# Three projection spans behind the last gate block, with SiLU built from Exp, and memory pools in another order

## The chip, the core and the metric

One core of a Trainium2 chip runs the whole kernel in one launch. The metric is the time on the device in microseconds (us). Three runs of the kernel before gave 1357.52, 1358.02 and 1362.52 us; their median, 1358.02 us, is the time before. The engines are named as the profile names them: PE (TensorE, matmuls and transposes), DVE (VectorE), ACT (ScalarE), POOL (GpSimd) and SP (SyncE, which here issues nearly all DMAs, in program order).

## The reference, cut to what matters

The layer normalises 2048 prompt tokens and 64 sample tokens, projects them with one weight matrix, runs differential attention and a convolution branch beside each other, multiplies each by its own gate, and projects the result back.

```python
h = rmsnorm(yp, norm_g[l])
q, k, v, g_att, u, g_conv = in_project(h, w_in[l])      # z = h @ w_in, split
o = lax.map(q_block, jnp.arange(n_blocks))              # diff_attend, causal, 128 queries each
att = attn_post(o, subln_g[l], lam_init)
conv, buf_p = conv_branch(u, zero_buf, *conv_p)         # depthwise conv, layernorm, silu, w_pw2
m = concatenate([att * silu(g_att), conv * silu(g_conv)], axis=-1)
yp = yp + m @ w_out[l]
```

All data are fp32. The change concerns `silu(g_conv)` for the last 128 of the 1024 gate channels, and the start of the attention.

## The kernel before, in words

**Phase 1** projects. The normalised input lies in SBUF, transposed, as a high and a low part (`hH`, `hL`) in four token groups of 512, 512, 512 and 576 tokens. `zmm` multiplies a block of 128 output channels with one span of tokens: 8 slices of the contraction times three products (high by high, low by high, high by low) are 24 matmuls that add up in one PSUM bank. A block has five spans (`SPANS`): three of 512 and two of 288 tokens. `zbank` takes the PSUM bank from a ring of pools, so that neighbouring spans lie in different banks. The last part of phase 1 is eight gate blocks. `gate_block(i)` computes for each span `zmm`, one ACT instruction `Silu` from PSUM into a tile `eF`, and one DMA of that tile to a DRAM tensor `gd[i]`. The layernorm of the convolution (`ln_steps`) runs between the spans of blocks 0 to 6.

**Phase 2** is attention. Scores `S` (lines 616 and 617) go from PE into two PSUM tiles of two banks each; DVE copies each to SBUF with a running minimum (lines 638 and 641); ACT takes the exponential (line 649); POOL and DVE combine the two softmaxes (lines 655 and 661); PE transposes (678), ACT copies (683), PE multiplies with the values (696). A group is one head and 512 queries. The first group (head 0, queries 0 to 511) has its keys `kt`, values `vt` and queries `qt` loaded during the gate blocks, into a pool of their own. Those of the second and third group (queries 512 to 1023 and 1024 to 1535) are loaded at the seam between the phases, from DRAM, into memory that `hH` and `hL` give back. `pw_stream` (weights `pwr`, split into `pwH` and `pwL`) is the pointwise convolution; it runs in low priority beside attention.

A scheduler sets the order of the instructions on each engine once, when the kernel is built: it follows the order in which the code records them, moved by `high_priority` offsets (a negative offset lets an instruction stand later). On the chip each engine and SP's DMA queue then go through their own list in that order, and an instruction whose semaphore is not yet up holds everything behind it on its engine. A PSUM or SBUF tile can be written again only after the last reader of its former content.

## Time and profile before

| | |
|---|---|
| median of three runs | 1358.02 us |
| profiled execution, its own time | 1358.04 us |
| its span, first to last instruction | 1356.3 us |
| PE busy | 1289.4 us, 95% of the span |
| DVE busy | 865.9 us, 64% |
| ACT busy | 517.2 us, 38% |
| mean granted PE clock | 0.989 |

The span is the time between the first and the last instruction of the profiled execution; its own time is 1.7 us longer. Times in the trace are microseconds from the start of the span. The seam between the phases lies at 692 us. A granted clock of 1.0 means 2.4 GHz for PE, and 0.5 means 1.2 GHz.

### The profile page before, as it was taken

What the parts mean: (1) busy time and instruction counts of PE and PEld (TensorE: products, weight loads), DVE (VectorE), ACT (ScalarE), POOL (GpSimd) and SP (SyncE); (2) the same over time, 40 slices, a digit from 0 to 9 for tenths busy, and PEclk for the clock granted to TensorE, in tenths of its full rate; (3) what the DMA queues carried; (4) which work ended last, traced back from release to release, by engine and by line L of the source; (5) the groups of instructions that cost most, each with busy time, mean ns of one, the idle gap of its engine ahead of it and who ended that gap; (6) DMA issues with size and microseconds to landing.
All of it is one profiled execution on the core that took longest, in us unless ns stands there. A gap on an engine that the chain in (4) does not pass through costs nothing.

```text
span 1356.3 us, 19981 instructions
## 1 busy us (share of the span) xinstructions
PE 1289.4 (95%) x7552; PEld 1105.1 (81%) x7552; DVE 865.9 (64%) x1215; ACT 517.2 (38%) x949; POOL 249.5 (18%) x353
## 2 busy tenths in 40 slices
PE   6999999999999999999988999999989779999997
PEld 5897998998888888888876888888877567767776
DVE  6623998998999992333137778777777935214332
ACT  6622111211212222323247666656767645212221
POOL 3200200200201100000024223224234425401110
PEclk9999999999999999999989999999999989999999
DMA  7632231330432336433166455363164544567731
GB/s 259 202 122 63 75 124 34 102 113 25 126 111 68 142 134 184 134 121 107 68 150 177 122 148 148 102 168 102 44 162 155 155 133 134 190 204 272 245 128 63
DMA packets 127858, 180.23 MB, mean 133 GB/s; under 512 B 25234, under 2 KB 74642, under 8 KB 127762
## 3 DMA queue, kind: packets, MB, share of 16 engines
q1 hardware_dynamic: 127762, 178.96, 43.8%
q8 instruction: 59, 0.97, 0.3%
q14 instruction: 37, 0.30, 0.1%
HBM read 113.88 MB, written 65.04 MB: 132 GB/s over the span
## 4 chain that ended last, share of the span: by engine, by line
PE 80%; DMA 8%; DVE 4%; ACT 2%; issue 2%; SPq 2%; POOL 1%; DVEq 0%; POOLq 0%; ACTq 0%
PE zps L204 39%; PE yps L974 13%; PE zps L328 7%; PE O L696 6%; PE pt L551 3%; PE S L616 3%; PE pt L678 3%; PE S L617 3%; DMA wor<-in_wout 2%; DMA kt<-kd 2%; DVE pL L661 1%; DVE pL L638 1%; DMA qt<-qd 1%; PE dO L763 1%; DMA wr<-in_wz 1%
## 5 line engine op out<-in xcount | busy, mean ns | idle before, releaser
L204 PE MATMUL zps<-hH,wH 128*128 128x512 f32 (+2 forms) x984 | 343.7, 350 | 3.9 <-ACT wH L160 3.9
L204 PE MATMUL zps<-hL,wH 128*128 128x512 f32 (+2 forms) x984 | 343.3, 349 | 0.0
L204 PE MATMUL zps<-hH,wL 128*128 128x512 f32 (+2 forms) x984 | 343.3, 349 | 0.0
L241 DVE SCALAR_TENSOR_TENSOR acc<-u,cst,acc 128x1024 f32<-128x1024 f32 x240 | 313.2, 1332 | 6.9 <-ACT acc L239 4.1
L204 PEld LDWEIGHTS zps<-hH,wH 128*128 128x128 f32 x984 | 185.5, 189 | 26.4 <-ACT wH L160 4.7
L204 PEld LDWEIGHTS zps<-hH,wL 128*128 128x128 f32 x984 | 185.7, 189 | 21.5
L204 PEld LDWEIGHTS zps<-hL,wH 128*128 128x128 f32 x984 | 185.4, 188 | 21.4
L974 PE MATMUL yps<-wo,mH 128*128 128x512 f32 x544 | 179.0, 404 | 6.2 <-ACT wo L1017 5.1
L616 PE MATMUL S<-kt,qt 128*128 128x512 f32 (+3 forms) x320 | 130.1, 410 | 20.3 <-DVE pL L638 6.9
L696 PE MATMUL O<-at,vt 128*128 128x256 f32 (+1 forms) x576 | 142.5, 375 | 0.6 <-ACT at L683 0.5
L974 PEld LDWEIGHTS yps<-wo,mH 128*128 128x128 f32 x544 | 101.9, 189 | 35.5 <-ACT wo L1017 5.3
L649 ACT ACTIVATE pL<-pL,mn 128x1152 f32<-128x1152 f32 (+7 forms) x64 | 104.3, 1630 | 37.3 <-DVE mn L641 36.9
L617 PE MATMUL S<-kt,qt 128*128 128x512 f32 (+3 forms) x320 | 114.3, 368 | 0.0
L696 PEld LDWEIGHTS O<-at,vt 128*128 128x128 f32 x576 | 103.1, 194 | 11.8 <-ACT at L683 1.1
L974 PE MATMUL yps<-wo,mL 128*128 128x512 f32 x272 | 108.5, 399 | 0.0
L683 ACT ACTIVATE at<-pt 128x512 f32<-128x512 f32 (+1 forms) x144 | 78.9, 567 | 56.0 <-PE pt L678 54.6
L616 PEld LDWEIGHTS S<-kt,qt 128*128 128x128 f32 x320 | 60.6, 190 | 41.2 <-DVE pL L638 11.2
L638 DVE TENSOR_SCALAR_CACHE_REDUCE pL<-S 128x1024 f32<-128x1024 f32 x64 | 78.1, 1220 | 23.1 <-PE S L617 22.5
L641 DVE CUSTOM_DVE_ANT_0 pS<-S,trim 128x768 f32<-128x768 f32 (+7 forms) x64 | 47.3, 754 | 63.0 <-PE S L617 61.1
L661 DVE SCALAR_TENSOR_TENSOR pL<-pL,cf,pL 128x512 f32<-128x512 f32 (+2 forms) x112 | 80.3, 774 | 10.5 <-POOL cf L656 10.2
L977 DVE TENSOR_TENSOR y<-yps,y 128x512 f32<-128x512 f32 (+1 forms) x34 | 23.2, 689 | 88.9 <-PE yps L974 66.0
L655 POOL TENSOR_TENSOR cf<-sm,mone 128x1 f32<-128x1 f32 x64 | 40.0, 625 | 215.8 <-ACT pL L649 112.6
(163 smaller groups left out, 1948.0 us busy)
## 6 DMA issues: line engine op xcount, KB each, us to landing
qt<-qd SPq DMA_DIRECT2D x32, 512.0 KB, 7.2
wr<-in_wz SPq DMA_DIRECT2D x48, 256.0 KB, 3.3
kt<-kd SPq DMA_DIRECT2D x38, 256.0 KB, 5.6
xt<-in_xp SPq DMA_DIRECT2D x16, 512.0 KB, 5.3
mf<-md SPq DMA_DIRECT2D x8, 1024.0 KB, 7.0
y<-in_xp SPq DMA_DIRECT2D x16, 512.0 KB, 5.0
kr<-in_ck SPq DMA_DIRECT2D x32, 256.0 KB, 4.5
vr<-in_cv SPq DMA_DIRECT2D x32, 256.0 KB, 4.9
```

The costliest lines, as they stand in the source:

```text
L204: PE.matmul(ps[:, 0:n], lhsT=wt[:, ks], rhs=ht[g][:, k, off:off + n], start=(i == 0), stop=(i == 3 * KC - 1))
L241: DVE.scalar_tensor_tensor(out=a, in0=u[:, t:t + HS], scalar=dwwt[:, cg, t:t + 1], in1=a, op0=ALU.mult, op1=ALU.add)
L328: PE.matmul(ps[0:n, 0:256], lhsT=ht[g][:, k, off:off + n], rhs=wt[:, sl], start=(i == 0), stop=(i == 3 * KC - 1))
L616: PE.matmul(ps[:, o:o + n], lhsT=t["mq"][:, m, qs_], rhs=kk, start=True, stop=False)
L617: PE.matmul(ps[:, o:o + n], lhsT=t["mq"][:, 2 + m, qs_], rhs=kk, start=False, stop=True)
L638: DVE.tensor_scalar(out=dst, in0=ps, scalar1=0.0, scalar2=None, op0=ALU.add, op1=ALU.min, accum_out=mn[:, m, 0:1])
L641: DVE.tensor_tensor_reduce(out=dst, in0=ps[:, 0:w], in1=trim[:, 1024 - w:] if diag else trim[:, 0:1].to_broadcast([P, w]), scale=1.0, scal ...
L649: ACT.activation(q, q, AF.Exp, bias=B["mn"][:, m, c:c + 1], scale=-1.0, accum_out=B["sm"][:, m, B["i"] % 4:B["i"] % 4 + 1])
L661: DVE.scalar_tensor_tensor(out=p0, in0=p1, scalar=B["cf"], in1=p0, op0=ALU.mult, op1=ALU.add)
L683: ACT.activation(at[:, 0:n * P], pt[:, 0:n * P], AF.Copy)
L696: PE.matmul(O[:, dst], lhsT=vt[j // 4][:, j % 4, :], rhs=at[:, src], start=(j == 0), stop=part)
L974: PE.matmul(ps, lhsT=m[:, k, sl], rhs=wo[k][x][:, cs], start=(i == 0), stop=(i == 3 * KC - 1))
```

## The change

`gate_block` gets an argument `late`. For the last block (i = 7) it is 3: the first two spans stay as they were, and the last three (512, 288 and 288 tokens; called late spans A, B and C from here) are recorded under `high_priority(offset=-LOW)`, with PSUM pool `psg` alone, which has one bank. Their SiLU is no longer one ACT instruction but a chain of four: Exp on ACT (from PSUM into `eF`), add 1 on DVE, reciprocal on DVE, and the product with the PSUM bank on DVE. The ACT table for Exp and Ln is loaded ahead of them instead of at the start of phase 2. The pools of both phases are opened in another order, so that the addresses of `hH`, `hL`, the weight ring and phase 2's tiles lie differently over each other. The rest of the code is the same.

```diff
-    hpool = ph1.enter_context(tc.tile_pool(name="hT", bufs=1))
     wpool = ph1.enter_context(tc.tile_pool(name="wring", bufs=3))
     wraw = ph1.enter_context(tc.tile_pool(name="wraw", bufs=2))
+    hpool = ph1.enter_context(tc.tile_pool(name="hT", bufs=1))
     epool = ph1.enter_context(tc.tile_pool(name="evac", bufs=5))
-    psz = ph1.enter_context(tc.tile_pool(name="psz", bufs=4, space=PSUM))
-    zps = [psz] * 4
-    hH = [hpool.tile([P, KC, n], F32R, name=f"hH{g}") for g, n in enumerate(GW)]
-    hL = [hpool.tile([P, KC, n], F32R, name=f"hL{g}") for g, n in enumerate(GW)]
+    psg = ph1.enter_context(tc.tile_pool(name="psg", bufs=1, space=PSUM))
+    psz = ph1.enter_context(tc.tile_pool(name="psz", bufs=3, space=PSUM))
+    zps = [psz, psz, psz, psg]
+    hH, hL = [None] * 4, [None] * 4
+    for g in (3, 0, 1, 2):
+        hH[g] = hpool.tile([P, KC, GW[g]], F32R, name=f"hH{g}")
+        hL[g] = hpool.tile([P, KC, GW[g]], F32R, name=f"hL{g}")
...
-    def gate_block(i, slots=()):
+    def gate_block(i, slots=(), late=0):
         w = wprep(wz[(8 if i < 4 else 16) + i])
-        for j, (g, off, n) in enumerate(SPANS):
+
+        def span(g, off, n, act):
+            ps = zmm(w, g, off, n)
+            f = ev(F32, "eF")
+            act(f[:, 0:n], ps[:, 0:n])
+            t0 = tokens(g, off)
+            SP.dma_start(gd[i][:, t0:t0 + n], f[:, 0:n])
+
+        def silu_exp(f, ps):
+            ACT.activation(f, ps, AF.Exp, scale=-1.0)
+            DVE.tensor_scalar(out=f, in0=f, scalar1=1.0, scalar2=None, op0=ALU.add)
+            DVE.reciprocal(out=f, in_=f)
+            DVE.tensor_tensor(out=f, in0=ps, in1=f, op=ALU.mult)
+
+        for sp in SPANS[0:len(SPANS) - late]:
             if len(slots):
                 for f in slots.pop(0):
                     f()
-            ps = zmm(w, g, off, n)
-            f = ev(F32, "eF")
-            ACT.activation(f[:, 0:n], ps[:, 0:n], AF.Silu)
-            t0 = tokens(g, off)
-            SP.dma_start(gd[i][:, t0:t0 + n], f[:, 0:n])
+            span(*sp, lambda f, ps: ACT.activation(f, ps, AF.Silu))
+        if late:
+            tc.keep_in_program_order(ACT.preload_act_table_set("natural_log_exp_and_others"))
+            zps[:] = [psg]
+            with tc.high_priority(offset=-LOW):
+                for sp in SPANS[len(SPANS) - late:]:
+                    span(*sp, silu_exp)
...
-        gate_block(i, slots)
+        gate_block(i, slots, 3 if i == 7 else 0)
...
+    st = pool2("st", 8)
     ppS = pool2("ppS", 1)
-    kp = pool2("kp", 2)
-    qp = pool2("qp", 2)
-    vp = pool2("vp", 2)
     ap_ = pool2("ap", AB)
     op = pool2("op", 2)
-    st = pool2("st", 8)
+    qp = pool2("qp", 2)
+    kp = pool2("kp", 2)
+    vp = pool2("vp", 2)
...
-    tc.keep_in_program_order(ACT.preload_act_table_set("natural_log_exp_and_others"))
```

How it moves the instructions is seen at three places. First PE, at the end of the last gate block. Before, the last matmuls `zps` of the block's last span stand directly ahead of the first four score matmuls `S`, and the second score pair (128x256) follows them:

```order
L204 MATMUL zps<-hH_138,wL 128x288
L204 MATMUL zps<-hL_142,wH 128x288
L616 MATMUL S<-kt_7066,qt 128x128 [waits DMAHW6_49,DMAHW3_49,DMAHW7_49,DMAHW2_49,Activation_49]
L616 MATMUL S<-kt_7066,qt 128x128 [waits DVE_49]
L617 MATMUL S<-kt_7066,qt 128x128 x2
L616 MATMUL S<-kt_7066,qt 128x256 [waits DVE_49]
L617 MATMUL S<-kt_7066,qt 128x256
```

Of the change, the end of late span A (512 columns) and the start of late span B (288 columns):

```order
L207 MATMUL zps<-hH_144,wH 128x512
L633 MATMUL S<-kt_7079,qt 128x128 [waits DMAHW6_49,DMAHW3_49,DMAHW7_49,DMAHW2_49,Activation_49]
L633 MATMUL S<-kt_7079,qt 128x128 [waits DVE_49,Activation_49]
L634 MATMUL S<-kt_7079,qt 128x128 x2
L207 MATMUL zps<-hH_144,wL 128x512
L207 MATMUL zps<-hL_145,wH 128x512
L207 MATMUL zps<-hH_138,wH 128x288 [waits DVE_49]
L207 MATMUL zps<-hH_138,wL 128x288
```

The first four score matmuls moved ahead of the last two matmuls of span A. All 48 matmuls of spans B and C follow without another instruction between them, and the second score pair (128x256) stands behind them, where it stood before. The first matmul of B, and likewise that of C, waits for DVE.

Second DVE, at the same place. `eF` is the SiLU chain, and the rows at L658 (before: L641) are the score minima of the first tiles:

```order
L355 TENSOR_SCALAR eF<-eF 128x512 [waits DMAHW0_49,Activation_49]
L356 RECIPROCAL eF<-eF 128x512 [waits DVE_49]
L357 TENSOR_TENSOR eF<-zps,eF 128x512 [waits DVE_49]
L355 TENSOR_SCALAR eF<-eF 128x288 [waits DMAHW2_49,DMAHW1_49,Activation_49]
L356 RECIPROCAL eF<-eF 128x288 [waits DVE_49]
L357 TENSOR_TENSOR eF<-zps,eF 128x288 [waits DVE_49]
L658 ISA pS_7103,mn<-S,trim 128x128 [waits PE_49]
L658 ISA mn 128x1
```

The chains of A and B stand ahead of the first score minimum; before, nothing of the gate block was on DVE there. The chain of C follows between the next minima.

Third SP's DMA queue, which stores the gate tiles `gd` and loads keys, values and queries. Before:

```order
L350 DMA gd_85<-eF 128x512 [waits DMAHW6_49,Activation_49]
L350 DMA gd_85<-eF 128x288 [waits DMAHW7_49,Activation_49]
L710 DMA kt_7074<-kd_64 64x2x512 [waits DMAHW0_49,PE_49]
L710 DMA kt_7074<-kd_64 64x2x512 [waits DMAHW1_49]
L712 DMA vt_7077<-vd 128x4x128 [waits DMAHW2_49,PE_49]
L719 DMA qt<-qd_60 64x4x512 [waits DMAHW3_49]
```

Of the change:

```order
L351 DMA gd_85<-eF 128x512 [waits DMAHW6_49,DVE_49]
L351 DMA gd_85<-eF 128x288 [waits DMAHW7_49,DVE_49]
L727 DMA kt_7087<-kd_64 64x2x512 [waits DMAHW0_49,PE_49]
L727 DMA kt_7087<-kd_64 64x2x512 [waits DMAHW1_49]
L729 DMA vt_7090<-vd 128x4x128 [waits DMAHW2_49,PE_49]
L736 DMA qt<-qd_60 64x4x512 [waits DMAHW3_49]
```

The loads of the second group keep their place behind the stores of spans A and B; those stores now wait for DVE's product instead of ACT's Silu. The PE wait of `vt` was for the last span (its memory was `hL3`) and is now for span A (`hH2`). Further down the queue the load of `pwr` moved behind the queries of the fourth group (it stood ahead of them), and on ACT the first split of `pwr` moved behind the first exponential of 1152 columns.

## Rows read from the trace of the kernel before

**Rows 1.** The page: busy time of each engine with its share of the span and instructions, and the chain of work that ended last, as shares of the span by engine and by line.

```profile
PE 1289.4 (95%) x7552; PEld 1105.1 (81%) x7552; DVE 865.9 (64%) x1215; ACT 517.2 (38%) x949; POOL 249.5 (18%) x353
...
PE 80%; DMA 8%; DVE 4%; ACT 2%; issue 2%; SPq 2%; POOL 1%; DVEq 0%; POOLq 0%; ACTq 0%
```

**Rows 2.** Windows around the seam. Columns: start and end, length; busy time of PE, PE's weight loads, DVE, ACT and POOL with the number of instructions; granted PE clock; busy share of the 16 DMA engines; GB/s.

```profile
680.50:692.40 11.90, 11.90 (x73) 10.78 (x71) 0.00 (x0) 1.60 (x3) 0.00 (x0) 1.00 0.21 68
692.40:698.70 6.30, 4.44 (x20) 2.59 (x19) 4.05 (x17) 5.68 (x16) 2.44 (x5) 1.00 0.99 216
698.70:702.30 3.60, 0.00 (x0) 0.00 (x0) 0.96 (x3) 1.23 (x4) 2.89 (x6) 0.64 1.07 226
702.30:706.30 4.00, 3.96 (x12) 3.43 (x13) 1.56 (x5) 0.63 (x1) 0.00 (x0) 0.50 1.13 206
706.30:719.90 13.60, 12.58 (x64) 9.36 (x62) 9.93 (x19) 10.29 (x22) 5.70 (x9) 0.99 1.02 235
719.90:727.00 7.10, 4.29 (x16) 3.34 (x16) 6.95 (x10) 3.68 (x6) 5.09 (x6) 0.76 1.00 226
```

**Rows 3.** PE in order of time: start, duration, line and operation with its tiles, and in brackets the idle time before it and what ended it. The first matmuls of the third, fourth and fifth span of the last gate block, then scores.

```profile
680.52 0.39 PE L204 MATMUL zps<-hH,wH 128*128 128x512 f32 x1
...
685.96 0.29 PE L204 MATMUL zps<-hH,wH 128*128 128x288 f32 x1
...
689.12 0.29 PE L204 MATMUL zps<-hH,wH 128*128 128x288 f32 x1
...
693.02 0.44 PE L616 MATMUL S<-kt,qt 128*128 128x128 f32 x2 [0.55 <-ACT eF L348]
693.30 0.38 PE L617 MATMUL S<-kt,qt 128*128 128x128 f32 x2
693.97 0.39 PE L616 MATMUL S<-kt,qt 128*128 128x256 f32 x1 [0.28 <-DVE mn L641]
...
698.25 0.44 PE L678 MATMUL pt<-ident,pS 128*128 128x128 f32 x2 [0.28 <-DVE pS L661]
702.34 1.19 PE L616 MATMUL S<-kt,qt 128*128 128x512 f32 x2 [3.65 <-DMA qt<-qd]
```

**Rows 4.** SP's queue in order of time: start, time over which it issued, line and DMA. The issues ahead of the seam, then the loads for the second group.

```profile
670.65 19.47 SPq L350 DMA_DIRECT2D gd<-eF  x5
690.21 1.26 SPq L710 DMA_DIRECT2D kt<-kd  x2
692.50 0.38 SPq L712 DMA_DIRECT2D vt<-vd  x1
692.92 1.25 SPq L719 DMA_DIRECT2D qt<-qd  x2
```

**Rows 5.** The chain of work that ended last, in order of time, from the last gate block to the first split of `pwr`: start, duration, what (short pieces left out).

```profile
679.77 12.71 PE zps L204 x76
...
696.43 11.90 DMA qt<-qd
...
708.40 9.16 DMA gd<-eF
...
717.58 4.53 DMA pwr<-in_wpw
...
722.13 1.06 ACT pwH L565
```

**Rows 6.** ACT in order of time, with the same columns as PE: the Silus of the last three spans, the table load, later an Exp of 512 columns and the first split of `pwr`.

```profile
686.21 0.60 ACT L348 ACTIVATE eF<-zps 128x512 f32<-128x512 f32 x1 [4.84 <-PE zps L204]
689.37 0.41 ACT L348 ACTIVATE eF<-zps 128x288 f32<-128x288 f32 x1 [2.56 <-PE zps L204]
692.56 0.41 ACT L348 ACTIVATE eF<-zps 128x288 f32<-128x288 f32 x1 [2.78 <-PE zps L204]
692.99 1.28 ACT L478 ACT_TABLE_LOAD   x1
694.28 0.40 ACT L649 ACTIVATE pS<-pS,mn 128x128 f32<-128x128 f32 x1
...
722.13 1.06 ACT L565 ACTIVATE pwH<-pwr 128x1024 fp32r<-128x1024 f32 x1 [2.40 <-DMA pwr<-in_wpw]
723.09 0.62 ACT L507 ACTIVATE rs<-rs 128x512 f32<-128x512 f32 x1
```

**Rows 7.** Groups of DVE instructions by line and shape: line, operation, output and input with shapes, count, busy us in total, mean ns of one, idle time before them.

```profile
L230 DVE TENSOR_TENSOR u<-zps,sg 128x512 f32<-128x512 f32 x12 | 8.3, 688 | 15.3 <-PE zps L204 14.9 <-issue 0.4
...
L395 DVE TENSOR_SCALAR dg<-ident,r 128x128 f32<-128x128 f32 x16 | 3.9, 284 | 6.1 <-POOL r L393 6.1
...
L789 DVE TENSOR_SCALAR Pn<-Pn,dsm 128x576 f32<-128x576 f32 x4 | 2.1, 520 | 0.1
L230 DVE TENSOR_TENSOR u<-zps,sg 128x288 f32<-128x288 f32 x4 | 1.8, 458 | 0.6 <-PE zps L204 0.5
...
L787 DVE RECIPROCAL dsm<-dsm 128x1 f32<-128x1 f32 x4 | 0.6, 161 | 0.1
L786 DVE TENSOR_TENSOR dsm<-dsm 128x1 f32<-128x1 f32 x4 | 0.6, 159 | 4.4 <-ACT Pn L785 4.4
...
L138 DVE TENSOR_SCALAR lamw<-ls 128x1 f32<-128x1 f32 x1 | 0.1, 142 | 0.0
```

## The prediction

> **What bounds the kernel now.** I read the page first. PE is busy for 95% of the span, and the chain that ended last lies on PE for 80% and on DMA for 8% [rows 1]. So time is won or lost where PE stands idle or runs at the low clock. The change touches one place of that kind, the seam at 692 us, so the windows there came next [rows 2]. The reader is to see that PE is full up to 692.4, idle for 1.9 of the next 6.3 us and for all of the 3.6 us after that, and then works 4.0 us at a clock of 0.50 (1.2 GHz); and that the DMA engines, at 0.21 until then, are full from 692.4 to 727. PE in order of time names the wait: the first scores of the second group start at 702.34, 3.65 us late, for the load of `qt` [rows 3]. The chain in order of time says what set that: PE until 692.5, then issues, `qt`, the store of the last gate tile, `pwr`, and at 722.13 ACT's split of `pwr` [rows 5]. Between 692 and 722 the kernel is bound by a stream of DMAs, and what matters there is when the stream starts. SP's queue shows that: five gate stores are issued until 690.12, `kt` follows at 690.21, `vt` at 692.50 and `qt` at 692.92 [rows 4].
>
> **The change, part by part.** The idea is that 11.8 us of gate matmuls fill the waits of the first group. The order does not let them: 48 of the 72 late matmuls stand in one piece ahead of the second score pair, and the first score minimum on DVE stands behind the chains of A and B. The first group starts no earlier, so I count nothing for filling. What the change adds is a wait: A, B and C share one PSUM bank, so B's first matmul waits until DVE has taken its product out of that bank, and C's until B's product is done. No other PE work lies in these two gaps. The store of B stands ahead of `kt` in SP's queue, so the DMA stream waits for B's chain too.
>
> *Span A.* It starts at 680.52 and ends where span B began, at 685.96 [rows 3]. The four score matmuls now inside it took from 693.02 to 693.68; I count 0.5, so PE is free at 686.5. Silu began 0.25 after the next span's first matmul (686.21 against 685.96) and took 0.60; an Exp of 512 columns took 0.62 [rows 6]. Exp of A thus runs from 686.75 to 687.35. The table load (1.28 us [rows 6]) lies in the 4.84 us that ACT waits for A, and costs nothing; before, it ended at 694.27 and the first exponential began at 694.28, with its minimum ready about 0.2 earlier, which is all that can be won there.
>
> *Add and product.* tensor_scalar took 284 ns at 128 columns and 520 ns at 576, 0.53 ns a column: 0.49 us at 512, 0.37 at 288. A product with a PSUM operand took 688 and 458 ns [rows 7]. Hand-overs between instructions are left out.
>
> *Reciprocal, the unknown.* The trace has it on one column only: 161 ns, against 142 for tensor_scalar and 159 for tensor_tensor on one column [rows 7]. If the difference is a fixed cost, 512 columns take what tensor_scalar takes, 0.5 us. If each column pays it, 2 to 19 ns a column come on top: 1.5 to 10.2 us at 512 columns. So the bounds are 0.5 and 10.2. I take 6 ns a column, the middle in ratio of 2 and 19: 0.5 + 3.1 = 3.6 us for A, 0.4 + 1.7 = 2.1 for B. The Trainium skill, page "VectorE: DVE Perf Modes", section "Walkthrough: the 8-slice pipeline in each mode", says that reciprocal is an iterative divide with a repeat count of 8. At the 0.96 GHz that the page gives, an estimate from it is 512 × 8 / 0.96 = 4.3 us for A and 2.4 for B, which would add 1.0 us to the sum below; the trace shows no reciprocal wide enough to check it.
>
> *Span B.* A's product ends at 687.35 + 0.5 + 3.6 + 0.7 = 692.15. PE has then been idle for 5.65 us. After the 3.6 idle us at 698.7 PE worked 4.0 us at clock 0.50, half of it lost: 2.0 us [rows 2]. I take the same after this longer gap. B takes 3.16 at full clock (689.12 − 685.96 [rows 3]) and so ends at 692.15 + 3.16 + 2.0 = 697.3. Its chain adds 0.25 + 0.41 (Silu of 288 columns, rows 6 has no Exp of this size) + 0.4 + 2.1 + 0.46 = 3.6, which is 700.9.
>
> *The DMA stream.* Before, Silu of the fourth span ended at 689.78 [rows 6] and `kt` was issued 0.43 later [rows 4]. Now `kt` goes out at 701.35, 11.1 us later. The other pool order wins some back: `vt` stood at 692.50, 1.03 after `kt` had been issued, waiting for the last span; its memory is now free after A. That leaves 10.1. Span C (3.16 us, again with some slow clock) and the first group's 4.7 us of scores (693.97 to 698.7 [rows 3]) end on PE at about 712 to 714, close to where `qt` now lands (702.34 + 10.1 = 712.4), so neither hides the other's delay.
>
> *Behind it.* The load of `pwr` stands further back, and its split stands behind an exponential. Before, ACT waited 2.40 us for it [rows 6]. The gain is between 0 and 2.4; I take 1.2, since the stream is as full as before. The early phase and the order within later attention groups shift by single instructions; I count them at nothing, give or take 3 us.
>
> Sum: 10.1 − 1.2 = 8.9 us on the profiled execution's 1358.04: **1366.9, so 1367 us**. That execution stands 0.02 above the median, so nothing is corrected.
>
> A rule of the Trainium skill speaks against the change too: "Perfetto Trace Analysis", section "Matmuls", says that independent matmul groups should rotate through different PSUM banks so that one's evacuation overlaps the next one's matmuls. This trace shows the rotating case, spans that follow with no idle time [rows 3]; by the rule the single bank costs the two chains, which is what the sum has.
>
> **The rivals.**
> *A cheap reciprocal* (0.5 and 0.4 us). A's product ends at 689.05; PE's gap is 2.55 us, and I take half the clock loss, 1.0. B ends at 693.2, its chain (1.9) at 695.1, and `kt` goes out at 695.55, 5.3 late. 5.3 − 1.0 − 1.2 = 3.1: 1361. For it: one column differs by only 2 ns from tensor_tensor. Against: nothing wide to go by.
> *A dear reciprocal* (19 ns a column: 10.2 and 5.9). A's product ends at 698.75, B's at 711.3, `kt` at 711.75: 21.5 − 1.0 − 1.2 = 19.3, 1377.
> *Not slower: the stall at 720 goes.* From 719.9 to 727.0 PE is busy for 4.29 of 7.1 us at a clock of 0.76 [rows 2]: 2.8 idle, and about half of 7.1 us at 1.2 GHz, up to 1.7 lost. ACT's wait for `pwr` stands ahead of attention's own work there [rows 5, 6]. If the new order takes all of it away (4.5 in place of 1.2) and the reciprocal is cheap, 5.3 − 1.0 − 4.5 = −0.2: 1358. It decides only if both hold; with the reciprocal as I take it the same gain gives 1364.
> *Faster: the filler fills.* All idle time from 692.4 to 702.3 (1.9 + 3.6) and the 2.0 of clock together are 7.5 us: 1350.5. Against it: PE's order puts B and C ahead of the second score pair, and DVE's puts the first minimum behind B. It could come only from gains elsewhere in the reordered attention.
>
> **How the numbers follow.** Chances: the forecast (1364 to 1370) 0.52; cheap reciprocal (1359 to 1364) 0.23; dear reciprocal or a low clock for longer 0.09; the stall at 720 gone 0.12; filler or other gains from the order 0.04. Below 0.5% (6.8 us; about what a measurement of this kernel can tell from no change) lie 1351.2 to 1364.8: the cheap reciprocal, most of the stall's case and a tenth of the forecast's, together 0.36. Faster gets 0.05, slower 0.59. The range 1357 to 1376 leaves out the filler's case, a little of the stall's, and the upper part of the dear reciprocal's; the forecast's own range is 1364 to 1370.
>
> **What would show it.** In the changed profile: two idle times of PE ahead of the matmuls of B and C, released by DVE's product (some 5.6 us for the first, 2.5 if the reciprocal is cheap); a granted clock of 0.5 in B; a reciprocal row of 512 columns, about 3.6 us; `kt` issued near 701 in place of 690; the wait for `qt` still ahead of the second group's scores; no `vt` wait between `kt` and `qt`; and a smaller wait of ACT for `pwr`. The prediction is wrong if `kt` leaves before 696, if B starts without a gap, or if the attention behind 727 takes another length than before by more than 3 us.

## The result

Four runs of the changed kernel have a median of 1373.64 us (1369.94 to 1377.92), four of the kernel before beside them 1358.39 (1357.52 to 1362.52): a ratio of 1.0109, 95% interval 1.0085 to 1.0133, so the change makes the kernel 1.1% slower. The profiled execution took 1369.94 us, the shortest of the four. Its span is 1368.2 us, 11.9 longer than before; the other 3 us of the difference between the medians lie within the spread of the four executions (8 us), and no trace shows them.

The page answers to [rows 1]: busy time, and the chain that ended last.

```profile
PE 1294.4 (95%) x7552; PEld 1107.4 (81%) x7552; DVE 877.8 (64%) x1224; ACT 517.1 (38%) x949; POOL 241.6 (18%) x353
...
PE 76%; DMA 11%; DVE 5%; ACT 3%; issue 3%; SPq 1%; POOL 1%; DVEq 0%; POOLq 0%; ACTq 0%
```

PE lost 4 points of the chain, DMA gained 3 and DVE 1. The seam in order of time, with the columns of [rows 3, 4, 6], engine by engine. First ACT: the last Silu of the block's first part, the table load, the Exps of A and B.

```profile
675.27 0.60 ACT L363 ACTIVATE eF<-zps 128x512 f32<-128x512 f32 x1 [4.89 <-PE zps L207]
675.88 1.28 ACT L365 ACT_TABLE_LOAD   x1
681.15 0.60 ACT L354 ACTIVATE eF<-zps 128x512 f32<-128x512 f32 x1 [3.99 <-issue]
692.53 0.41 ACT L354 ACTIVATE eF<-zps 128x288 f32<-128x288 f32 x1 [10.78 <-PE zps L207]
```

DVE: the chains of A and B, and the first score minimum.

```profile
681.78 0.43 DVE L355 TENSOR_SCALAR eF<-eF 128x512 f32<-128x512 f32 x1 [18.83 <-ACT eF L354]
682.24 3.35 DVE L356 RECIPROCAL eF<-eF 128x512 f32<-128x512 f32 x1
685.63 0.69 DVE L357 TENSOR_TENSOR eF<-zps,eF 128x512 f32<-128x512 f32 x1
692.98 0.31 DVE L355 TENSOR_SCALAR eF<-eF 128x288 f32<-128x288 f32 x1 [6.65 <-ACT eF L354]
693.32 1.95 DVE L356 RECIPROCAL eF<-eF 128x288 f32<-128x288 f32 x1
695.31 0.46 DVE L357 TENSOR_TENSOR eF<-zps,eF 128x288 f32<-128x288 f32 x1
695.68 0.28 DVE L658 CUSTOM_DVE_ANT_0 pS<-S,trim 128x128 f32<-128x128 f32 x1
```

PE: the first matmuls of B and C, and the first scores of the second group.

```profile
686.38 0.61 PE L207 MATMUL zps<-hH,wH 128*128 128x288 f32 x1 [5.31 <-DVE eF L357]
...
695.82 0.61 PE L207 MATMUL zps<-hH,wH 128*128 128x288 f32 x1 [3.37 <-DVE eF L357]
...
707.76 0.76 PE L633 MATMUL S<-kt,qt 128*128 128x512 f32 x1 [0.57 <-DMA qt<-qd]
```

SP's queue: the gate stores, then the loads of the second group.

```profile
665.15 30.96 SPq L351 DMA_DIRECT2D gd<-eF  x5
696.20 1.25 SPq L727 DMA_DIRECT2D kt<-kd  x2
697.58 0.52 SPq L729 DMA_DIRECT2D vt<-vd  x1
698.14 1.24 SPq L736 DMA_DIRECT2D qt<-qd  x2
```

The chain of span A is Exp (0.60), add (0.43), reciprocal (3.35) and product (0.69); PE stands idle for 5.31 us until the product of A is out of the bank, and for 3.37 until that of B is. DVE's first score minimum starts at 695.68, right behind B's product, though its scores were computed at 680. `kt` leaves at 696.20, and the second group's scores start at 707.76. The windows of the same stretch (columns as in [rows 2]) are cut where spans end:

```profile
675.00:686.40 11.40, 6.09 (x30) 4.79 (x28) 4.47 (x3) 2.48 (x3) 0.00 (x0) 0.96 0.06 23
686.40:692.40 6.00, 6.00 (x24) 5.76 (x24) 0.00 (x0) 0.00 (x0) 0.00 (x0) 0.51 0.12 44
692.40:695.80 3.40, 0.05 (x1) 0.00 (x0) 2.76 (x4) 0.41 (x1) 0.00 (x0) 0.98 0.00 0
695.80:700.60 4.80, 4.78 (x25) 4.78 (x26) 0.38 (x4) 0.00 (x0) 0.00 (x0) 0.66 0.56 161
700.60:707.80 7.20, 4.06 (x17) 2.24 (x16) 6.33 (x18) 4.48 (x16) 2.68 (x6) 0.87 1.08 227
```

B (686.4 to 692.4) ran at 0.51 (1.2 GHz) nearly throughout, C at 0.66 on average.

To see where the 11.9 us lie, the table cuts each trace at four points: ACT's Silu of the last block's second span (the last work that the change leaves alone), the first score matmul of the second group, the first and the last `rs` (ACT's logarithm in the normalisation of a group; there are 16 groups), and the end. What lies behind the last `rs` is called the output phase: the attention of the sample tokens (the sampled decode, which reads its cache in pages) and the projection back. The last column tells whether the loads that open this decode (`smt` and what follows) stand on SP ahead of or behind the last group's store `md<-gate`. Ratios are against the kernel before, run beside each on the same chip. Times are in us; the rows e1 to e12 are the experiments below.

| kernel | ratio (95% interval) | Silu, second span | to second group's scores | to first `rs` | first to last `rs` | last `rs` to end | `smt` |
|---|---|---|---|---|---|---|---|
| before | 1 | 680.77 | 21.6 | 36.8 | 451.1 | 187.6 | ahead |
| after | 1.0109 (1.0085–1.0133) | 675.27 | 32.5 | 48.1 | 451.4 | 193.4 | behind |
| e1 layout only | 1.0010 (0.9977–1.0044) | 674.53 | 21.0 | 37.1 | 448.5 | 193.7 | behind |
| e2 attention pools only | 1.0034 (1.0005–1.0063) | 677.83 | 23.4 | 39.3 | 447.5 | 195.4 | behind |
| e3 after, old attention pools | 1.0082 (1.0056–1.0108) | 674.80 | 31.6 | 47.8 | 456.2 | 191.0 | ahead |
| e4 after, stores on ACT | 1.0076 (1.0049–1.0103) | 675.66 | 32.3 | 47.0 | 449.6 | 192.6 | behind |
| e5 projection layout only | 0.9982 (0.9967–0.9998) | 674.76 | 21.4 | 37.4 | 452.8 | 188.5 | ahead |
| e6 = e5, stores on ACT | 0.9991 (0.9975–1.0008) | 675.62 | 17.8 | 37.0 | 452.3 | 190.3 | ahead |
| e7 after, Ln chain | 1.0063 (1.0034–1.0092) | 674.54 | 27.4 | 38.9 | 456.9 | 191.7 | behind |
| e8 after, two banks | 1.0133 (1.0094–1.0173) | 675.82 | 25.5 | 46.8 | 452.5 | 193.7 | behind |
| e9 after, far bank | 1.0050 (1.0027–1.0072) | 676.60 | 25.3 | 45.8 | 446.1 | 192.2 | behind |
| e10 = e9, Ln chain, old pools | 0.9983 (0.9966–1.0000) | 674.24 | 23.4 | 36.6 | 454.4 | 188.7 | ahead |
| e11 bank split only | 0.9975 (0.9956–0.9994) | 675.29 | 21.3 | 37.1 | 452.0 | 188.6 | ahead |
| e12 = e10, stores on ACT | 0.9991 (0.9971–1.0010) | 674.30 | 19.7 | 31.4 | 458.8 | 188.4 | ahead |

From before to after: 5.5 us won ahead of the seam, 11.3 lost in it (48.1 − 36.8), 0.3 lost in attention, 5.8 lost in the output phase: −5.5 + 11.3 + 0.3 + 5.8 = 11.9. The prediction had the second of these terms and counted the others at nothing.

The first term is seen in PE's waits of the first 120 us (engine, line, what it waited for: us in total, times, longest), before and then after:

```profile
PE zps L204 <- ACT wH L160: 3.9, 2, 2.2
```

```profile
PE zps L207 <- ACT wH L163: 0.4, 1, 0.4
```

Early weights (`wH`) came late twice before and hardly now: 3.5 us. From 24 to 32 us, behind the first of these waits, the granted clock was 0.79 on average in the trace of before and 1.00 in that of after, worth another 1.7 us. The last term is seen on SP, around the end of attention, before and then after:

```profile
1159.35 3.58 SPq L729 DMA_DIRECT2D smt<-in_smask  x8
...
1171.99 0.33 SPq L510 DMA_DIRECT2D md<-gate  x1
```

```profile
1177.46 0.32 SPq L527 DMA_DIRECT2D md<-gate  x1
1177.87 3.62 SPq L746 DMA_DIRECT2D smt<-in_smask  x8
```

Before, the loads of the decode were issued 12.6 us ahead of the last group's gate store. In the changed kernel they stand behind that store, which waits for POOL's product. PE then waits in the output phase for cache pages (`vr`), for which it did not wait before:

```profile
PE dO L780 <- DMA vr<-in_cv: 3.0, 6, 1.8
```

The rest of the 5.8 us is longer work: the same 1183 matmuls kept PE busy there for 181.9 us instead of 178.9, at a granted clock of 0.982 instead of 0.988.

### The profile page after: what moved, and what is told of

Read it like the earlier page. It is cut to its first block, busy times and chain, and to the rows that moved or that the text cites. A ratio compares the mean times of both kernels' runs of the same rounds, so it can differ in the third digit from the quotient of the medians.

```text
span 1368.2 us, 19994 instructions
## 1 busy us (share of the span) xinstructions
PE 1294.4 (95%) x7552; PEld 1107.4 (81%) x7552; DVE 877.8 (64%) x1224; ACT 517.1 (38%) x949; POOL 241.6 (18%) x353
## 4 chain that ended last, share of the span: by engine, by line
PE 76%; DMA 11%; DVE 5%; ACT 3%; issue 3%; SPq 1%; POOL 1%; DVEq 0%; POOLq 0%; ACTq 0%
PE zps L207 37%; PE yps L991 11%; PE zps L331 7%; PE O L713 6%; PE pt L568 3%; PE S L633 3%; PE pt L695 3%; PE S L634 3%; DMA wor<-in_wout 2%; DMA kt<-kd 2%; DVE pL L678 1%; DMA xt<-in_xp 1%; DMA vr<-in_cv 1%; DVE pL L655 1%; ACT pL L666 1%
## 5 line engine op out<-in xcount | busy, mean ns | idle before, releaser
L207 PEld LDWEIGHTS zps<-hH,wL 128*128 128x128 f32 x984 | 186.9, 190 | 21.3
L207 PEld LDWEIGHTS zps<-hL,wH 128*128 128x128 f32 x984 | 186.7, 190 | 21.3
L666 ACT ACTIVATE pL<-pL,mn 128x1152 f32<-128x1152 f32 (+7 forms) x64 | 104.3, 1629 | 31.8 <-DVE mn L658 31.6
L633 PEld LDWEIGHTS S<-kt,qt 128*128 128x128 f32 x320 | 61.2, 191 | 38.2 <-DVE pL L655 12.6
L672 POOL TENSOR_TENSOR cf<-sm,mone 128x1 f32<-128x1 f32 x64 | 37.2, 581 | 231.4 <-ACT pL L666 116.8
L331 PE MATMUL zps<-wH,hL 128*128 128x256 f32 (+1 forms) x272 | 76.9, 283 | 0.0
```

The lines of the kernel that those rows point to most:

```text
L207: PE.matmul(ps[:, 0:n], lhsT=wt[:, ks], rhs=ht[g][:, k, off:off + n], start=(i == 0), stop=(i == 3 * KC - 1))
L331: PE.matmul(ps[0:n, 0:256], lhsT=ht[g][:, k, off:off + n], rhs=wt[:, sl], start=(i == 0), stop=(i == 3 * KC - 1))
L633: PE.matmul(ps[:, o:o + n], lhsT=t["mq"][:, m, qs_], rhs=kk, start=True, stop=False)
L666: ACT.activation(q, q, AF.Exp, bias=B["mn"][:, m, c:c + 1], scale=-1.0, accum_out=B["sm"][:, m, B["i"] % 4:B["i"] % 4 + 1])
```

## The experiments

The theory behind the first four was that of three places: an early gain from the layout, the loss at the seam from the late spans, and the loss in the output phase from the order of the decode's loads.

**e1: the layout without the late spans.** Against after:

```diff
-        gate_block(i, slots, 3 if i == 7 else 0)
+        gate_block(i, slots)
```

with the table load back at the start of phase 2.

> The kernel of after with all five spans of the last gate block left where they were before (Silu, the table load behind them); the new order of the hidden-state tensors, the separate PSUM bank and the new order of the attention pools stay. Theory of three places: the layout alone brings the early gain (the Silu of block 7's second span at 675.3 instead of 680.8), the late spans alone bring the loss at the seam (10.9), and the output phase loses where the loads that open the sampled decode (smt) stand on SP behind the last group's gate store; here they stand ahead of it, as before. So 1358.4 - 5.5 = 1353, with kt issued near 684.7 and the second group's scores near 697. Rival: the late spans pull the early part up too (they change the whole order), and the layout alone is worth nothing: 1358.

Measured: ratio 1.0010. The early gain is there (674.53), and the seam is that of before. SP's queue, and PE at the second group's first scores:

```profile
683.98 1.25 SPq L728 DMA_DIRECT2D kt<-kd  x2
```

```profile
695.49 1.19 PE L634 MATMUL S<-kt,qt 128*128 128x512 f32 x2 [3.01 <-DMA qt<-qd]
```

In one point the expectation was wrong: `smt` stands behind the last gate store in this kernel too, and the output phase takes 193.7 us as in after. So the time is that of before, as the rival had it, but not for its reason: the early gain came without the late spans and was lost again in the output phase. The late spans alone make the seam's loss, and that of the output phase is there without them.

**e2: the order of the attention pools alone**, in the kernel before.

```diff
+    st = pool2("st", 8)
     ppS = pool2("ppS", 1)
-    kp = pool2("kp", 2)
-    qp = pool2("qp", 2)
-    vp = pool2("vp", 2)
     ap_ = pool2("ap", AB)
     op = pool2("op", 2)
-    st = pool2("st", 8)
+    qp = pool2("qp", 2)
+    kp = pool2("kp", 2)
+    vp = pool2("vp", 2)
```

> The kernel before with one edit: the attention pools in the order of after (st, ppS, ap, op, qp, kp, vp). Early phase and gate block as before. In this build the smt loads stand on SP behind the last group's gate store, as in after. Theory of three places: the output phase alone loses 5.8, so 1358.4 + 5.8 = 1364, with smt some 3 us behind the last rs instead of 9 us ahead of it. Rival one: the loss in the output phase comes from the late spans, and this kernel runs at 1358. Rival two: the later start of the sampled decode is not what costs the time; smt comes late and the time stays within 2 us of 1358.

Measured: 1.0034. SP's queue around the end of attention, and PE's wait for `vr` in the output phase of this kernel:

```profile
1167.34 0.32 SPq L510 DMA_DIRECT2D md<-gate  x1
1167.75 3.62 SPq L729 DMA_DIRECT2D smt<-in_smask  x8
```

```profile
PE dO L763 <- DMA vr<-in_cv: 4.0, 9, 1.5
```

The pool order alone puts `smt` behind the store and brings the waits for `vr`; the output phase takes 195.4 us instead of 187.6. The first `rs` comes 2.5 us later (`kt` left 11.7 us behind the Silu instead of 9.4), and from there to the last `rs` it is 3.6 us shorter, so that about half of the output phase's loss comes back. What the pool order costs as a whole is the ratio: 0.0034, some 4.6 us. This kernel has the projection phase of before, in the same order, and yet its Silu came at 677.83 instead of 680.77: its early waits for `wH` were 2.7 us instead of 3.9, and its clock from 24 to 32 us was 1.00 instead of 0.79. So 2.9 of the 5.5 us of the early term can be the spread from run to run.

**e3: after with the old attention pools** (e2's edit, the other way round).

> The kernel of after with the attention pools in the order of before (ppS, kp, qp, vp, ap, op, st); late spans, hidden-state order and PSUM bank as in after. In this build the smt loads stand ahead of the last group's gate store. Theory of three places: the output phase gets its 5.8 back and nothing else moves: 1373.6 - 5.8 = 1368, kt near 696, second group's scores near 708. Rival: the new pool order is what keeps kt's memory free of the late spans, and the old one puts kt later still: 1374 or more.

Measured: 1.0082, against 1.0109 for after (the intervals overlap); the output phase gets 2.4 of its 5.8 us back, the seam stays (47.8). Attention is 4.8 us longer, so the part of the theory that nothing else moves was wrong. Over all traces of the table the output phase takes 191.7 to 195.4 us where `smt` stands behind, 187.6 to 191.0 where it stands ahead. But `smt` stands behind in exactly the kernels with the new pool order, and no run moves these loads alone: that their place is the cause is argued from PE's waits for `vr`, not shown.

**e4: after with the last block's five stores on ScalarE's queue.**

```diff
-            SP.dma_start(gd[i][:, t0:t0 + n], f[:, 0:n])
+            (ACT if i == 7 else SP).dma_start(gd[i][:, t0:t0 + n], f[:, 0:n])
```

> The kernel of after with one edit: the five gate stores of the last block are issued from ScalarE's queue instead of SP's, so that the loads of the second group (kt, vt, qt) stand behind no late store on SP. Theory that the seam's loss is the SP queue: kt is issued near 682 instead of 696.2, qt no longer ends a wait of PE, the second group's scores start some 8 to 11 us earlier than 707.8, and the time is 1363 to 1366. Rival: the waits of PE for DVE's product (5.3 + 3.4 us) and the half clock behind them are the loss by themselves; kt comes early, the second group's scores move by under 3 us, and the time is 1371 to 1374. A third way: the stores now hold ScalarE up in front of the score exponentials (they wait for DVE's product), and the seam gets longer: above 1375.

Measured: 1.0076, its interval overlapping that of after. The rows are of SP's queue (`kt`), of DVE (B's product and the first minimum) and of PE (the second group's first scores):

```profile
675.66 1.26 SPq L727 DMA_DIRECT2D kt<-kd  x2
```

```profile
694.99 0.46 DVE L357 TENSOR_TENSOR eF<-zps,eF 128x288 f32<-128x288 f32 x1
695.37 0.28 DVE L658 CUSTOM_DVE_ANT_0 pS<-S,trim 128x128 f32<-128x128 f32 x1
```

```profile
707.94 0.62 PE L633 MATMUL S<-kt,qt 128*128 128x512 f32 x1
```

`kt` left 20.5 us earlier than in after, and PE no longer waited for `qt`. But the second group's scores started at 707.94, 32.3 us behind the Silu instead of 32.5. The first group's minima stand behind B's chain on DVE in any case, and the second group's scores behind the first group. The rival was right in its mechanism: `kt` came early and the second group's scores moved by 0.2 us. Its time was not: against before, the ratio stands for 1368.7 us, between the theory's range and the rival's. In after the second group's `qt` landed at 707.63, and the first group's scores ended at 706.8: the late stream of loads and the late first group cost nearly the same time side by side, and taking away the one leaves the other.

**e5, e6 and e11: which part of the layout wins.** e5 is the kernel before with the projection phase's pools of after (order of `hH` and `hL`, and the bank of its own); e6 adds e4's edit; e11 has the bank alone:

```diff
-    psz = ph1.enter_context(tc.tile_pool(name="psz", bufs=4, space=PSUM))
-    zps = [psz] * 4
+    psg = ph1.enter_context(tc.tile_pool(name="psg", bufs=1, space=PSUM))
+    psz = ph1.enter_context(tc.tile_pool(name="psz", bufs=3, space=PSUM))
+    zps = [psz, psz, psz, psg]
```

> The kernel before with the layout of the projection phase alone from after: hidden-state tensors behind the weight rings in the order 3, 0, 1, 2, and one of the four accumulator banks in a pool of its own. All five spans of the last gate block as before, attention pools as before. Theory of three places: the early phase is 5 to 6 us shorter (kt near 684 instead of 690), the sampled decode is opened ahead of the last group's gate store as before, and the whole kernel is 3 to 6 us faster than before: 1350 to 1353 beside a kernel before of 1356. Rival: the early gain is lost again behind the seam, as in the run of the whole layout without late spans (which came to a ratio of 1.001): 1355 to 1358.

> The same kernel with the last gate block's five stores issued from ScalarE's queue. Theory: with Silu on ScalarE the store follows its own engine and waits for nothing, SP has kt some 8 us earlier (near 676), PE's wait of 3.0 to 3.65 us for qt at the second group goes, and the time is 3 to 5 us below the kernel without this edit. Rival: the loads of the second group then share the queues with the stores and land as late as before; or the first group's softmax, which starts when the last span ends in both, sets the pace: within 1.5 us of the kernel without this edit.

> The kernel before with one edit: one of the four accumulator banks of the projection phase in a pool of its own (three and one, in the same rotation). Hidden-state tensors, gate block and attention pools as before. Theory that the early gain comes from the order of the early weight loads, which in this build is that of after on SP: kt near 684 to 685, PE busy 100 of 100 us from 100 to 200, and time 1350 to 1355 beside 1356 to 1358 for before. Rival: the early gain comes with the place of the hidden-state tensors; kt near 690 and time as before.

Measured: 0.9982, 0.9991 and 0.9975. e11 has the lowest ratio of the study, 0.25% below before. For e5 the theory's 3 to 6 us came out as 2.4 (1355.7 us, in the rival's range). e11 has the whole early gain; PE in its second 100 us (columns as in [rows 2]) is full, where it was busy for 98.3 before:

```profile
100.00:200.00 100.00, 100.00 (x676) 93.35 (x675) 77.65 (x73) 20.39 (x39) 7.91 (x6) 1.00 0.29 84
```

So the bank split changes the order of the early weight loads (up to 660 us SP, PE, ACT and DVE go through the same list in e11 as in after), and the place of `hH` and `hL` adds nothing that can be measured. e6 issued `kt` at 670.17 and reached the second group's scores 17.8 us behind the Silu instead of 21.4, but its first `rs` at 37.0, about where e5 has it, because ACT's first split of `pwr` stands right ahead of that `rs` in this build and waited 4.53 us for its load. Both the theory (a gain) and the rival (loads that land as late) missed this wait.

Four kernels now form a square: e5 and e1 without the late spans, e3 and after with them; e5 and e3 with the old order of the attention pools, e1 and after with the new one. The late spans raise the ratio by 0.0100 with the old order and by 0.0099 with the new, 13.5 us. The pool order raises it by 0.0028 and 0.0027, 3.7 us, and the projection layout lowers it by 0.0018; these two steps are no larger than the intervals, that of the late spans is far clear of them. In the traces, counted from the Silu, the late spans put the first `rs` 10.4 and 11.0 us later and the last 13.9 in both pairs: some 3 us more are lost within attention, and no run shows on what.

**e7: the chain without DVE's reciprocal.** Against after:

```diff
             ACT.activation(f, ps, AF.Exp, scale=-1.0)
-            DVE.tensor_scalar(out=f, in0=f, scalar1=1.0, scalar2=None, op0=ALU.add)
-            DVE.reciprocal(out=f, in_=f)
+            ACT.activation(f, f, AF.Ln, bias=1.0)
+            ACT.activation(f, f, AF.Exp, scale=-1.0)
             DVE.tensor_tensor(out=f, in0=ps, in1=f, op=ALU.mult)
```

> The kernel of after with 1/(1+e) worked out on ScalarE as Exp(-Ln(1+e)), so that VectorE has one product per span instead of an add, a reciprocal and a product. Chain theory: PE's wait ahead of B is 5.3 - 3.8 + 1.2 = 2.7 instead of 5.3, that ahead of C 3.4 - 2.3 + 0.8 = 1.9 instead of 3.4, the first group's score minima on VectorE start 4 us earlier than 695.7, kt is issued near 692, and the time is 4 to 6 us below after's 1373.6. Rival: a gap of any length halves the clock of the span behind it and the loss is there, not in the length of the chain: under 2 us of gain.

Measured: 1.0063. PE's two waits, and the chain of work that ended last (start, us, what) at the point where the gain shrinks again:

```profile
683.13 0.40 PE L207 MATMUL zps<-hH,wH 128*128 128x288 f32 x1 [2.78 <-DVE eF L357]
...
689.93 0.40 PE L207 MATMUL zps<-hH,wH 128*128 128x288 f32 x1 [1.94 <-DVE eF L357]
```

```profile
707.45 10.45 DMA gate<-gd
```

The waits are 2.78 and 1.94 us, as the chain theory had them, and the first `rs` comes 9 us earlier than in after (38.9 against 48.1). The gate tile is then waited for, whose load takes 10.45 us among the others, and at the second `rs` nothing of the 9 us is left (71.6 us behind the Silu, 69.4 in after); attention is 5.5 us longer than in after. So the chain's length is the price at the seam (the loads and the first group both stand behind it), and more than half of what is won there is lost again behind it. The rival holds in part: behind these shorter waits B and C still took 4.9 us each at a granted clock of 0.66, where B took 6.1 in after.

**e8 and e9: a second bank.** e8 gives the late spans two neighbouring banks (`psg` with two buffers, `psz` with two). e9 takes the second one from the far end:

```diff
-    zps += [ph1.enter_context(tc.tile_pool(name="psx", bufs=2, space=PSUM))] * 2
+    psx = ph1.enter_context(tc.tile_pool(name="psx", bufs=2, space=PSUM))
+    zps += [psx] * 2
...
-            zps[:] = [psg]
+            zps[:] = [psg, psx]
```

> The kernel of after with two PSUM banks in the late spans' pool (and two instead of three in the other), chain as in after with the reciprocal on VectorE. Chain theory: PE goes from A to B without a wait, C waits only for A's product; B is no longer at half clock; the wait of 5.3 and most of 3.4 go. VectorE is then the limit: its products end at 686.3 (A), 689 (B), 692 (C), the first minimum follows near 690 to 692 instead of 695.7, and the time is 4 to 7 us below after's 1373.6. Rival (VectorE's queue, not PE's waits, is what sets the seam, since the minima stand behind the reciprocals in any case): the first minimum stays behind all of the late spans' work on VectorE and the gain is under 2 us.

> The kernel of after with a second bank for the late spans, this time one of the two at the far end of PSUM, which the attention phase gives to its transposes and outputs and not to the first score tiles: A and C on the pool's own bank, B on the far one. Reciprocal on VectorE as in after. Theory that in the run with two neighbouring banks the gain was lost because the second bank is the one that the first scores want: here B follows A without a wait, C waits for A's product (686.3), the first minimum stands behind B's product near 689 instead of 695.7, and the first rs comes near 716 instead of 723.3; time 1366 to 1369 beside after's 1373.6. Rival: the score minima of the first group stand behind reciprocals on VectorE in any case and the gain is under 2 us.

Measured: 1.0133 for e8, 1.0050 for e9: e8 gains nothing against after, as its rival had it, and e9 0.0059, 8.0 us, the theory's gain and a little more. In both B follows A without a wait, and PE's wait ahead of C falls to 2.19 us; but in e8 a new one of 3.38, released by C's product, stands ahead of the first scores, where in e9 they were computed at 681. PE's rows of e8 (C, then the first scores), then of e9 (C, then the second group's first scores):

```profile
686.52 0.40 PE L207 MATMUL zps<-hH,wH 128*128 128x288 f32 x1 [2.19 <-DVE eF L357]
...
694.87 0.69 PE L633 MATMUL S<-kt,qt 128*128 128x128 f32 x2 [3.38 <-DVE eF L357]
```

```profile
687.74 0.40 PE L207 MATMUL zps<-hH,wH 128*128 128x288 f32 x1 [2.19 <-DVE eF L357]
...
701.85 0.67 PE L634 MATMUL S<-kt,qt 128*128 128x512 f32 x1 [2.70 <-DMA qt<-qd]
```

One of e8's two banks, that of A and C, is one that the first score tile needs: C's product ended at 694.82 and the scores followed at 694.87. So the wait moved from the late spans to the scores. In both, the second group's scores start 7 us earlier than in after, and the first `rs` only 1 to 2. What holds it is on ACT, in the waits between 705 and 730 us of e9:

```profile
ACT pwH L583 <- DMA pwr<-in_wpw: 6.8, 2, 4.7
...
PE pt L696 <- ACT rs L524: 5.9, 1, 5.9
```

The first split of `pwr` stands ahead of the first `rs` in these two kernels as in e6 (behind it in after), and `pwr`'s load waits for the last gate store to land. Both expectations missed this. Why e8 and e9 lie 11 us apart in their medians the traces show in part only: 6.4 us lie in attention between the first and the last `rs`, where the two builds have other orders.

**e10: three mendings together**, the far bank, the Ln chain and the old attention pools.

> The kernel of after with three mendings at once: the far bank of the run before, 1/(1+e) as Exp(-Ln(1+e)) on ScalarE, and the attention pools in the order of before. Theory that the late spans cost what their chain, their bank and the order of the sampled decode's loads cost, and nothing else: A's product near 682.5, B's near 686, C right behind; first minimum near 686, kt near 687, first rs near 710, which is 2 us ahead of the kernel with the projection layout alone (712.1); time 1352 to 1356. Rival: the seam is then set by the stream of loads behind kt (the DMA share is at its full value from 700 to 725 in every run), as where the Ln chain's 10 us at the first rs fell to 3 us two groups later because the gate tile was still on its way: time 1359 to 1363.

Measured: 0.9983, the same as e5 and e11. The seam, on PE (the second group's first scores) and in POOL's waits:

```profile
697.59 1.19 PE L634 MATMUL S<-kt,qt 128*128 128x512 f32 x2 [4.24 <-DMA qt<-qd]
```

```profile
POOL osb L526 <- DMA gate<-gd: 4.2, 1, 4.2
```

A, B and C now run without a gap, and the first group's work on DVE starts at 685.02. The late spans no longer cost anything that can be measured, and they still win nothing: the time that they make free goes into a wait of 4.24 us for `qt`, where before it was 3.65 [rows 3], and into one of 4.2 for the gate tile, where it was 2.7; the second `rs` comes 7.0 us later behind the Silu than before (67.1 against 60.1). The theory's time was right and so was the rival's mechanism.

**e12: e10 with the stores on ScalarE's queue** (e4's edit).

> The kernel with the three mendings (far bank, Ln chain, old attention pools) and the last gate block's stores on ScalarE's queue. Theory that the mended seam is set by the stream of loads behind kt: SP can issue kt near 676 instead of 685.5, PE's 4.2 us wait for the second group's qt goes, the gate tile of the first group lands some 8 us earlier, the second rs comes near 735 instead of 741, and the time is 3 to 6 us below the 1355.5 of the kernel without this edit, below every version so far. Rival: the memory of the second group's tiles comes free only with the late spans (they still read the hidden state), so the loads behind the first kt start no earlier, and the time is within 1.5 us of 1355.5.

Measured: 0.9991, no gain over e10. SP's queue:

```profile
668.86 1.26 SPq L728 DMA_DIRECT2D kt<-kd  x2
...
674.72 1.53 SPq L737 DMA_DIRECT2D qt<-qd  x2
684.89 5.04 SPq L728 DMA_DIRECT2D kt<-kd  x2
```

The wait for `qt` is gone and the first `rs` comes 31.4 us behind the Silu, 5.4 less than before: here the filler does fill. By the last `rs` all of it is lost: the way from the first to the last takes 458.8 us, the longest of all. The rival holds in part: `kt` and `qt` of the second group went out 17 and 13 us earlier than in e10 (685.54 and 687.48 there), but the loads behind them only 4 (684.89 against 688.76): the next two `kt` loads left at 684.89 and 689.36, each right behind the landing of a late gate store (684.88 and 689.34), which released it; so on ScalarE's queue too the stores hold the stream. The lead over before, 5.4 us at the first `rs`, is 3.1 at the second, 1.7 at the third and nothing at the seventh. What takes it no run shows; this build has another order of instructions there.

## Why the prediction was right, and where not

**The seam: near in amount.** A's chain was to hold PE for 5.65 us; it did for 5.31. The reciprocal was taken at 3.6 and 2.1 us; it took 3.35 and 1.95. (The estimate of 4.3 and 2.4 from the Trainium skill, "VectorE: DVE Perf Modes", section "Walkthrough: the 8-slice pipeline in each mode", was too long; the rows decide.) B was to lose 2.0 us to the clock; at 0.51 nearly throughout it took 6.0 instead of 3.16, a loss of 2.8. `kt` was to leave 11.1 us later, counted from the start of the late spans; it left 11.5 later (20.9 behind the second span's Silu, 9.4 before). `vt`'s wait was to go, and went. The second group was to start 10.1 us later, and started 10.9 later (32.5 against 21.6). Two signs of being wrong were named here: B did not start without a gap, and `kt` left at 696.20, just behind the 696 that was the limit; that limit was a time in the trace, and the early gain had moved the whole seam 5.5 us ahead.

**The seam: half of the reason.** The prediction held that what matters between 692 and 722 is when the stream of loads starts. e4 shows that this alone is not so: with `kt` 20 us earlier the second group starts at the same time, because the first group's minima stand behind B's chain on DVE. The prediction said of DVE that the minimum stands behind those chains, and of PE that its work ends close to where `qt` lands; it did not see that either of the two parties was enough for nearly all of the loss.

**`pwr`: wrong.** 1.2 us were to come back. ACT's split still waited 2.49 us, at 730.20, against 2.40 [rows 6]: its load went out as much later as the stream did.

**Early phase and later groups: counted at nothing, and large.** This step failed in opposite directions: 5.5 us won early (e11: by the bank split; 2.9 of it within the spread of one kernel), 5.8 lost in the output phase (e2: by the order of the attention pools, probably through the place of the decode's loads on SP). That the sum came out near is luck in this part: the two nearly cancel. Attention itself changed by 0.3 us, and that is a balance too: by the square of e5, e1, e3 and after the late spans lengthen it by 3.4 and 2.9 us, and the new pool order shortens it by 4.3 and 4.8. The prediction gave 3 us either way for the early phase and the later attention, and did not name the output phase. By the same square the late spans alone cost 13.5 us, where the whole sum was 8.9.

**The rule on banks.** The Trainium skill, "Perfetto Trace Analysis", section "Matmuls", asks for independent matmul groups to rotate through PSUM banks. The trace agrees where the second bank is free for it: in e9 B follows A without the 5.31 us wait. In e8 B follows A as well, but one of its two banks is wanted by the next phase, and 3.38 us of wait come back ahead of the first scores.

**The median.** It is 6.6 us above the forecast of 1367, inside the range of 1357 to 1376 and outside the narrower 1364 to 1370. In the trace, the sum of the terms gives 11.9 where 8.9 was forecast.

**What stays open.** Attention from the first to the last `rs` takes between 446.1 and 458.8 us in these builds, with the same work. The old pool order goes with the longer times (451.1 to 458.8), but the Ln chain in the new order has 456.9. What in a build makes it so no run shows, and e12's lost 5 us are among it. Nor does a run shorten the chain and leave the loads late, which would be the other half of e4.

## What to carry to other kernels

Work moved into a stall as filler helps only if it stands behind the work that it is to fill in on every engine's list, and has a PSUM bank that nothing near it wants; one slow instruction in its chain on a shared in-order engine (here a reciprocal of 3.35 us) moves the stall instead of filling it. When a seam has two late parties side by side, mending one can give nothing until the other is mended too (here 0.2 of 10.9 us). And an edit of pools changes the order far from the place that it is for: look at what moves in the first and the last phase, above all which loads stand behind a store that waits, before counting them at nothing.

## What was not expected of the hardware

A reciprocal on DVE took 3353 ns at 128x512 and 1951 at 128x288, 6.3 ns a column, twelve times the slope of the add on the same tiles (427 and 310 ns, 0.52 ns a column). Exp(−Ln(1+e)) on ACT came out shorter: PE's wait ahead of B fell from 5.31 to 2.78 us. After that 5.31 us wait PE ran nearly all of B at 1.2 GHz, 6.1 us from first start to last end instead of 3.3; in e3, behind a wait of the same 5.31 us, B took 4.8 at a mean granted clock of 0.67. So what the clock costs behind one wait differed by 1.2 us between two runs.
